# Sixteen repeated semaphore waits at the head of ScalarE's and VectorE's programs

## The chip, the cores and the metric

The kernel runs on one core of one Trainium2 chip. The metric is the device time of one execution in microseconds (us). The median of three runs of the kernel before is 160.86 us (160.74 to 161.05).

## The reference

```python
def reference(x):                     # x: 32 x 512 x 1024, float32
    relu_x = np.maximum(x, 0)
    return np.sum(relu_x, axis=-1).astype(np.float32)   # 32 x 512
```

Seen as a matrix, x has 16384 rows of 1024 numbers, 64 MiB in all. Each row's positive numbers are summed to one number. There is no matrix product: the work is to read 64 MiB once, and to make one pass of relu and one pass of summing over it.

## The kernel before, in words

**Tiling.** The 16384 rows are laid over the 128 partitions, 128 rows for each partition. The work goes by "rows of a partition": one such row is a piece of 128 partitions x 1024 numbers, 512 KB. There are 7 big chunks of 16 rows (`CHUNKS`, 8 MB each), then a tail of 8, 4 and 2 rows (`TAIL`), and then the last two rows, which are cut into four small pieces (`first`, `second`, `third` and the `seam` tile), so that little work is left when the last bytes arrive.

**Loads.** All loads are DMAs that SyncE (SP) issues on one queue. The buffer `buf` has three slots (`NB = 3`) of 16 rows. Chunk 0 is loaded by two DMAs (1 row and 15 rows) on the same semaphore, `s_in[0]`, so that chunk 0 has landed when `s_in[0]` is at 32; the kernel moves these two issues ahead of the core's opening barrier (L95 to L97). Chunks 1 and 2 follow at once. From chunk 3 on, the issue at L91 waits at L87 until VectorE has finished the chunk that used the slot (`s_dve` at `done[c - NB]`). The tail's issues (L101), the pieces of the last rows (L112) and the seam (L115) come behind the wait for VectorE's end of chunk 4.

**Work.** For chunks 0 to 5 ScalarE (ACT) does relu in place in large ACTIVATEs (L145, one ACTIVATE for the whole of chunk 0, then steps of 7 and 9 rows and smaller), and each raises `s_act`. VectorE (DVE) waits for `s_act` (L159) and sums the rows with TENSOR_REDUCE (L160), each raising `s_dve`. Of chunk 5, four rows are done with relu and sum in one instruction: two on ScalarE by `on_act` (L127), two on VectorE by `on_dve` (L130). From chunk 6 on, nothing passes between the two engines any more: they take alternate rows, each with relu and sum in one instruction. At the very end both wait for the seam and for each other's halves (L199 to L203), SP stores the last results (L207), and waits until the stores have landed (L209).

**Order at the start.** ScalarE's first instruction of the kernel's body is the table load for relu, put in by the compiler (it shows as ACT_TABLE_LOAD under L145). Then comes the ACTIVATE of chunk 0, which itself carries the wait of L140 for `s_in[0]` at 32. VectorE's first instruction is the first TENSOR_REDUCE of chunk 0, which carries the wait for `s_act` at 1. Each engine takes its own instructions in order.

A wait that is followed by an instruction of its engine rides on that instruction; where there are more waits than one, the compiler makes EVENT_SEMAPHORE instructions of them, which only wait, two waits to one instruction (L122 and L209 are such pairs on SP).

Of the kernel before, what the change touches and what calls it, by code (L numbers as in the profile page):

```python
# [8 lines left out]
CHUNKS = [[(0, 0, 1), (1, 0, 15)]] + [[(1, 16 * c + 15, 16)] for c in range(6)]  # L9
# [2 lines left out]
TAIL = [8, 4, 2]  # L12
CUT = 912
HEAD = 256


def bass_relu_sum_kernel(
# [19 lines left out]
    B, S, _ = x.shape  # L37
# [14 lines left out]
    w = D - CUT  # L52
    seam = nc.alloc_sbuf_tensor("seam", [P, 2 + w + HEAD + 2], fp32)
    res = nc.alloc_sbuf_tensor("res", [P, J], fp32)
# [3 lines left out]
    s_in = [nc.alloc_semaphore(f"s_in{i}") for i in range(n_in)]  # L58
# [11 lines left out]
    sp, act, dve = nc.sync, nc.scalar, nc.vector  # L70
# [38 lines left out]
    flat = buf[:, tb, r : r + 2, :].rearrange("p j d -> p (j d)")  # L109
    first, second, third = [(0, CUT), (D + D // 2, 2 * D), (D + HEAD, D + D // 2)]  # L110
    for k, (lo, hi) in enumerate((first, second, third)):
        sp.dma_start(out=flat[:, lo:hi], in_=rows[:, lo:hi]).then_inc(  # L112
            s_in[NBIG + len(TAIL) + k], 16
        )
    sp.dma_start(out=seam[:, 2 : 2 + w + HEAD], in_=rows[:, CUT : D + HEAD]).then_inc(s_seam, 16)  # L115
    sp.wait_ge(s_turn, 1)
# [9 lines left out]
    def on_act(t, acc):  # L126
        return act.activation(t, t, AF.Relu, accum_out=acc)  # L127

    def on_dve(t, acc):
        return dve.tensor_scalar(  # L130
            out=t, in0=t, scalar1=0.0, scalar2=None, op0=ALU.max, op1=ALU.add, accum_out=acc
        )

    def row(c, i):
        return buf[:, c % NB, i, :], res[:, c * BIG + i : c * BIG + i + 1]

    k = 0
    for c in range(NTWO):
        alone = BIG - sum(ACT_STEPS[c])
# [54 lines left out]
    act.wait_ge(s_in[-2], 16)  # L194
    on_act(flat[:, lo:hi], seam[:, k + HEAD : k + HEAD + 1]).then_inc(s_seam, 1)
    lo, hi = third
    dve.wait_ge(s_in[-1], 16)
    on_dve(flat[:, lo:hi], seam[:, k + HEAD + 1 : k + HEAD + 2]).then_inc(s_seam, 1)
    act.wait_ge(s_seam, 16 + 2)  # L199
    act.wait_ge(s_half, 2)  # L200
    on_act(seam[:, 0:k], res[:, J - 2 : J - 1]).then_inc(s_last, 1)
    dve.wait_ge(s_seam, 16 + 2)
    on_dve(seam[:, k : k + HEAD + 2], res[:, J - 1 : J]).then_inc(s_last, 1)  # L203

# [33 lines left out]
```

## Time and profile before

| What | Value |
|---|---|
| median of 3 runs | 160.86 us (160.74 to 161.05) |
| profiled execution: span, first to last instruction | 159.4 us |
| profiled execution: last semaphore record of the closing barrier, from the span's start | 160.85 us |
| DVE busy | 120.6 us (76%), 59 instructions |
| ACT busy | 101.5 us (64%), 54 instructions |
| loads and stores (q1), share of 16 DMA engines | 98.1% |
| HBM read | 67.11 MB, 421 GB/s over the span |
| code (q14) within the span | 1 packet of 8192 bytes, at 159.21 us |

The page's span goes from SP's first DMA issue to SP's last wait. Behind it lies the closing of the program: the engines meet in a barrier, clear their semaphores and meet once more. The last record of this in the trace is at 160.85 us, 1.46 us behind the span's end, so the profiled execution's own time, counted like this, agrees with the median of the runs.

A line such as `137.72 1.22 DVE L130 ... [0.42 <-DMA buf<-in_x_dram]` of the timeline says: at 137.72 us VectorE began an instruction of line 130 that took 1.22 us; the engine was idle for 0.42 us before it, and a load's landing ended that idle time. In the view of waits, the three numbers are the total, the number of waits and the longest. In the table by stretch, the last three columns are the granted clock, the busy share of the DMA engines and GB/s. "q" behind an engine's name means its sequencer, the part that takes the instructions in order and handles waits.

### The profile page before, as it was taken

How to read it: one execution, taken by the hardware profiler on the slowest of the kernel's cores; microseconds unless marked ns; L12 is line 12 of the kernel's file. 1: busy time of each engine (PE TensorE's matmuls, PEld its weight loads, DVE VectorE, ACT ScalarE, POOL GpSimd, SP SyncE). 2: the span in 40 equal slices, each digit the busy share in tenths (PEclk: the TensorE clock that was granted, in tenths of full speed). 3: DMA queues.
4: the chain of work that ended last, by engine and by line, in shares of the span. 5: the costliest groups of instructions: out<-in, count | busy, mean ns of one | idle time of the engine just before them, and what ended most of it. 6: DMA issues, size and time to landing. Idle time of an engine off the chain costs nothing.

```text
span 159.4 us, 150 instructions
## 1 busy us (share of the span) xinstructions
DVE 120.6 (76%) x59; ACT 101.5 (64%) x54; POOL 0.2 (0%) x4
## 2 busy tenths in 40 slices
DVE  0000000009999999999999999999999999898995
ACT  3000059980799708996099941999329980496975
POOL 0000000000000000000000000000000000000000
DMA  9997996996996997989979969969969979798994
GB/s 378 493 401 339 493 526 263 526 526 263 526 493 296 526 444 345 526 378 411 526 312 477 526 263 526 526 263 526 526 263 526 444 345 526 321 469 374 417 400 142
DMA packets 2457, 67.18 MB, mean 421 GB/s; under 512 B 536, under 2 KB 792, under 8 KB 1176
## 3 DMA queue, kind: packets, MB, share of 16 engines
q1 hardware_dynamic: 2456, 67.18, 98.1%
q14 instruction: 1, 0.01, 0.0%
HBM read 67.11 MB, written 0.07 MB: 421 GB/s over the span
## 4 chain that ended last, share of the span: by engine, by line
DVE 55%; DMA 34%; ACT 9%; SPq 2%; issue 0%
DVE res L160 54%; DMA buf<-in_x_dram 34%; ACT buf L145 9%; SPq L101 1%; SPq L112 1%; DVE buf L130 0%; DVE seam L130 0%; SPq L91 0%; DVE turned L169 0%
## 5 line engine op out<-in xcount | busy, mean ns | idle before, releaser
L160 DVE TENSOR_REDUCE res<-buf 128x4 f32<-128x4096 f32 (+3 forms) x18 | 99.4, 5596 | 35.5 <-ACT buf L145 35.5
L145 ACT ACTIVATE buf<-buf 128x7168 f32<-128x7168 f32 (+5 forms) x13 | 80.4, 6233 | 46.1 <-DMA buf<-in_x_dram 46.1
L127 ACT ACTIVATE buf<-buf 128x1024 f32<-128x1024 f32 (+2 forms) x19 | 19.0, 999 | 8.9 <-DMA buf<-in_x_dram 8.9
L130 DVE TENSOR_SCALAR_CACHE_REDUCE buf<-buf 128x1024 f32<-128x1024 f32 (+2 forms) x19 | 20.7, 1143 | 1.7 <-DMA buf<-in_x_dram 1.6
L127 ACT ACTIVATION_READ_ACCUMULATOR buf<-buf 128x1 f32 x19 | 3.6, 188 | 0.0
L145 ACT ACT_TABLE_LOAD x1 | 1.3, 1283 | 1.3 <-PEq L223 1.3
L130 DVE DVE_READ_ACCUMULATOR buf<-buf 128x1 f32 x19 | 1.6, 84 | 0.0
L130 DVE TENSOR_SCALAR_CACHE_REDUCE seam<-seam 128x258 f32<-128x258 f32 x1 | 0.4, 421 | 0.0
L127 ACT ACTIVATE seam<-seam 128x114 f32<-128x114 f32 x1 | 0.3, 300 | 0.1
L169 DVE STREAM_TRANSPOSE turned<-res 128x32 f32<-128x32 f32 x1 | 0.2, 211 | 0.0
L127 ACT ACTIVATION_READ_ACCUMULATOR seam<-seam 128x1 f32 x1 | 0.2, 186 | 0.0
L223 POOL MEMSET const-bfloat16-1.0<- 128x1 bf16 x1 | 0.1, 101 | 0.0
L223 POOL MEMSET const-uint8-127<- 128x1 uint8 x1 | 0.1, 101 | 0.0
L223 POOL MEMSET const-float32-0.0<- 128x1 f32 x1 | 0.1, 98 | 0.2 <-issue 0.2
L223 POOL MEMSET const-float32-1.0<- 128x1 f32 x1 | 0.1, 98 | 0.0
L130 DVE DVE_READ_ACCUMULATOR seam<-seam 128x1 f32 x1 | 0.1, 82 | 0.0
## 6 DMA issues: line engine op xcount, KB each, us to landing
buf<-in_x_dram SPq DMA_DIRECT2D x1, 7680.0 KB, 21.1
buf<-in_x_dram SPq DMA_DIRECT2D x1, 4096.0 KB, 25.3
buf<-in_x_dram SPq DMA_DIRECT2D x1, 2048.0 KB, 29.9
buf<-in_x_dram SPq DMA_DIRECT2D x1, 1024.0 KB, 31.9
buf<-in_x_dram SPq DMA_DIRECT2D x1, 512.0 KB, 3.3
buf<-in_x_dram SPq DMA_DIRECT2D x1, 456.0 KB, 32.5
buf<-in_x_dram SPq DMA_DIRECT2D x1, 256.0 KB, 32.7
seam<-in_x_dram SPq DMA_DIRECT2D x1, 184.0 KB, 32.6
```

The costliest lines, as they stand in the source:

```text
L101: sp.dma_start(out=buf[:, tb, r : r + n, :], in_=xv[-1][:, r : r + n, :]).then_inc(s_in[NBIG + i], 16)
L112: sp.dma_start(out=flat[:, lo:hi], in_=rows[:, lo:hi]).then_inc(s_in[NBIG + len(TAIL) + k], 16)
L127: return act.activation(t, t, AF.Relu, accum_out=acc)
L130: return dve.tensor_scalar(out=t, in0=t, scalar1=0.0, scalar2=None, op0=ALU.max, op1=ALU.add, accum_out=acc)
L145: act.activation(t, t, AF.Relu).then_inc(s_act, 1)
L160: dve.tensor_reduce(out=res[:, c * BIG + r : c * BIG + r + n], in_=buf[:, c % NB, r : r + n, :], axis=X, op=ALU.add,).then_inc(s_dve, 1)
L169: dve.transpose(out=turned[:, :], in_=res[:, 0:32]).then_inc(s_turn, 1)
L223: nc = _bacc.Bacc("TRN2", target_bir_lowering=False, num_devices=1)
```

## The change

A constant `FILL = 16` is added, and, behind the definition of `row` (L134 and L135) and ahead of the loop that emits both engines' work (L138), ScalarE and VectorE get sixteen waits each for `s_in[0]` at 32, that is, for the landing of both loads of chunk 0. They become eight instructions on each engine. ScalarE's own wait of L140 for the same value stays. Nothing else changes.

```diff
+FILL = 16
...
     def row(c, i):
         return buf[:, c % NB, i, :], res[:, c * BIG + i : c * BIG + i + 1]
 
+    for engine in (act, dve):
+        for _ in range(FILL):
+            engine.wait_ge(s_in[0], 16 * len(CHUNKS[0]))
     k = 0
     for c in range(NTWO):
```

## Prediction

> **What bounds the kernel now.** I read the table by stretch first, with cuts where chunks land. Its last columns are clock, DMA share and GB/s.
>
> ```profile
> 21.60:41.00 19.40, 5.50 (x2) 13.89 (x2) 0.00 (x0) 1.00 1.00 432
> 60.30:79.70 19.40, 19.36 (x6) 13.99 (x3) 0.00 (x0) 1.00 1.00 432
> 99.00:118.40 19.40, 19.40 (x5) 14.08 (x4) 0.00 (x0) 1.00 1.00 432
> 147.40:152.30 4.90, 4.65 (x8) 4.27 (x8) 0.00 (x0) 1.00 0.97 416
> ```
>
> The loads run at 432 GB/s with the DMA engines full, early and late. DVE (first number) looks full in the middle too, so the waits have to say which of the two is ahead.
>
> ```profile
> ACT buf L145 <- DMA buf<-in_x_dram: 46.1, 6, 19.1
> DVE res L160 <- ACT buf L145: 35.5, 1, 35.5
> DVE buf L130 <- DMA buf<-in_x_dram: 1.6, 4, 0.5
> ```
>
> ACT waits for a load at every chunk. DVE waits once at the start and then works without a gap, because it starts late and catches up; from chunk 6 on it, too, waits for loads, four times. ACT's timeline gives the pace of the loads:
>
> ```profile
> 1.27 1.28 ACT L145 ACT_TABLE_LOAD   x1 [1.27 <-PEq L223]
> 21.61 13.86 ACT L145 ACTIVATE buf<-buf 128x16384 f32<-128x16384 f32 x1 [19.06 <-DMA buf<-in_x_dram]
> 40.97 13.95 ACT L145 ACTIVATE buf<-buf 128x7168 f32<-128x7168 f32 x2 [5.50 <-DMA buf<-in_x_dram]
> 60.31 13.95 ACT L145 ACTIVATE buf<-buf 128x7168 f32<-128x7168 f32 x2 [5.39 <-DMA buf<-in_x_dram]
> ```
>
> A chunk lands every 19.35 us; ACT needs 13.95 us for one, DVE 17.3 us (52.75 to 70.07). So **the stream of loads sets the end**. The chain of waits puts 54% on DVE's L160, but it follows the tail's issue (L101, at 122.07 us) back to DVE, and that issue had time: the queue was full with chunk 6, which landed at 137.72 us.
>
> **The change, part by part.** Of each engine's sixteen waits, made into eight EVENT_SEMAPHOREs, the first blocks until chunk 0 has landed (21.59 us, the semaphore's last count), so all eight pass after that, in order.
>
> *DVE's eight* cost nothing on the path: behind them stands the first TENSOR_REDUCE, which waits for ACT until 35.50 us anyway. The cover is 13.9 us, against at most 8 x 0.079 = 0.63 us (below).
>
> *ACT's eight* stand ahead of the ACTIVATE of chunk 0, for which DVE waits. The trace of before has no row of such a string on ACT. Bounds for one: below, ACT's only EVENT_SEMAPHOREs last 0.017 us (L223, L200); above, POOL's two at the start begin 0.079 us apart (1.070 and 1.149), the second waiting for nothing. Nearest in kind is SP's L122, with two waits: it begins at 157.005, and the next instruction at 157.080, 0.075 us apart. I take 0.075: 8 x 0.075 = 0.60 us (0.14 to 0.63).
>
> *The table load* is moved by the change, though the diff doesn't name it. Now it runs at 1.27 us, behind ACT's opening barrier and ahead of the ACTIVATE that carries the wait, and is hidden under the first load (19.06 us of idle time follow). It belongs to L145, to the ACTIVATE; the new waits are instructions of their own ahead of that line. I expect the load behind them, in the open: 1.283 us, plus 0.055 us as between ACT's barrier instruction (1.194 + 0.017) and the load (1.266). What passes between a table load's end and an ACTIVATE no row shows, since a wait follows it; at least 0, and, by the longest pause for draining in the trace (POOL's DRAIN), 0.179 us. I take 0.
>
> ```profile
> L145 ACT ACT_TABLE_LOAD  x1: 1283/1283/1283, 1.3 to 1.3; - x1
> ```
>
> The Trainium skill bears on both halves of this. "ScalarE: Activation LUTs", section "Step-by-step: what each stage is for", says that the compiler places the load right before the ACTIVATE that needs it; that speaks against this change. Its section "What ACT_TABLE_LOAD costs" adds a drain of about 1380 ns to the 1283 ns; the trace has the 1283 ns, and no run here shows the other. By that page the sum below would be 3.32 us instead of 1.94, and the time some 162.1 us.
>
> Sum: ACT begins chunk 0 later by 0.60 + 0.06 + 1.28 = **1.94 us** (0.14, if the load stays ahead and each wait costs 0.017, to 0.63 + 0.06 + 1.28 + 0.18 = 2.15).
>
> *Where that goes.* ACT ends chunk 0 at 35.47 + 1.94 = 37.41, ahead of chunk 1 at 40.97: ACT is on time again after one chunk. DVE starts at 35.50 + 1.94 and, having no gap up to 137.2 us, stays 1.94 late. Queued behind it are SP's issues. Chunk 3's, at 52.86 us, goes to 54.8; the queue still holds chunk 2 until 60.3, so the DMA engines don't run dry. The later ones have more room, each chunk 19.35 - 17.3 = 2 us more. Then come DVE's gaps at the end:
>
> ```profile
> 137.72 1.22 DVE L130 TENSOR_SCALAR_CACHE_REDUCE buf<-buf 128x1024 f32<-128x1024 f32 x1 [0.42 <-DMA buf<-in_x_dram]
> ...
> 147.43 1.22 DVE L130 TENSOR_SCALAR_CACHE_REDUCE buf<-buf 128x1024 f32<-128x1024 f32 x1 [0.51 <-DMA buf<-in_x_dram]
> ...
> 152.32 1.22 DVE L130 TENSOR_SCALAR_CACHE_REDUCE buf<-buf 128x1024 f32<-128x1024 f32 x1 [0.24 <-DMA buf<-in_x_dram]
> ...
> 157.01 0.42 DVE L130 TENSOR_SCALAR_CACHE_REDUCE buf<-buf 128x256 f32<-128x256 f32 x1 [0.40 <-DMA buf<-in_x_dram]
> ```
>
> An instruction of DVE can begin 0.08 us before the record of the one ahead ends (39.834 against 35.497 + 4.419). So the gaps are 137.72 - 137.22 = 0.50, 147.43 - 146.85 = 0.58, 152.32 - 152.00 = 0.32, 154.84 - 154.61 = 0.23 and 157.01 - 156.53 = 0.48: together 2.11 us. 1.94 us of delay is used up there, piece by piece, with 0.17 to spare when the third piece lands. The end stays: span 159.4, closing barrier to 160.85. That is the profiled execution's own time; the median of the runs is 160.86. At the upper bound 2.15 - 2.11 = 0.04 us is left over. Without these gaps, the whole 1.94 us would show.
>
> *Code.* Eight instructions more on each engine move all that follows. The trace has one code packet within the span:
>
> ```profile
> q14 instruction: 1, 0.01, 7.7%
> ```
>
> (in the DMA view from 159.0 to 159.4 us): 8192 bytes, begun at 159.212, lasting 0.493 us. I take it to stay off the path, and make it a rival.
>
> **The rivals.**
>
> *1. The load stays ahead of the waits (0.12).* For it: nothing keeps a table load from running early. Against: it bears the ACTIVATE's line. Then the delay is 0.14 to 0.63 us, used up in DVE's first two gaps: 160.86.
>
> *2. Slower: after the table load something is in the way that the trace hides (0.15).* Its place is between the load and the first ACTIVATE; now 19.06 us of idle time cover whatever is there. It decides from 2.11 - 1.94 = 0.17 us on; beyond that, each ns of it is a ns of the end. The far row is the load itself: as long again is 1.283 us, 1.283 - 0.17 = 1.11 us late, 161.97. Over 0.49 us of it the change is slower by over 0.2%.
>
> *3. The code packet comes earlier (0.17).* It begins 1.3 us after DVE's and ACT's last instructions (157.9); SP's DMAs take about a us from issue to their first packet (0.00 to 1.01, 157.93 to 158.77), so it is likely asked for when one of the two leaves its work. Eight instructions earlier on either is about 155.8 us or before, and the packet then falls among the last loads, which land up to 156.99. One of the 16 engines would be busy for 0.493 us with it, and a landing needs all 16. Price 0 to 0.49: up to 161.35. Against: at 156 us little is left on the queue. The skill's "Runtime: NRT & Kernel Launch", "Instruction fetch mechanics", has refills of 16 KiB, mostly hidden; the trace shows 8192 bytes, and by that rule the price would be 0.
>
> *4. Faster: the closing now waits for that packet (0.11).* It ends at 159.705, while the barrier's release runs from 159.51 to 159.67. Asked for earlier, it frees at least 0.19 us (159.705 - 159.51), at most its 0.49: 160.37. Against: the barrier's records follow each other at about 0.04 us, with no hole where one engine is late.
>
> **How the numbers follow.** The likeliest is that ACT's delay is absorbed: 0.45, at 160.86 (to 160.90 at its bounds). Rival 1 adds 0.12 at the same time. About 0.2% (0.32 us) is what a measurement of this kernel can tell from no change. Of rival 3's 0.17, 0.10 are over that, 0.07 not; of rival 4's 0.11, 0.08 and 0.03; rival 2 is over it. Within: 0.45 + 0.12 + 0.07 + 0.03 = 0.67; slower 0.15 + 0.10 = 0.25; faster 0.08. The range goes from 160.5 (rival 4's larger part left out) to 161.5 (rival 3 whole, and the first part of rival 2); what it leaves out is under 0.2.
>
> **What would show it.** Right: ACT_TABLE_LOAD at 22.2 us or so; the first ACTIVATE at 23.5; the first TENSOR_REDUCE at 37.4; ACT's second chunk at 40.97 as before; the waits of L130 on loads down from 1.6 us to near nothing; chunks landing every 19.35 us. Wrong in a step: the load still at 1.27 (rival 1); a hole between load and ACTIVATE (rival 2); q14's packet before 157 us (rival 3); a shorter stretch behind the span (rival 4). The prediction falls altogether if chunks land at another pace, or if DVE loses its 2 us of catching up in a chunk.

## The result

The changed kernel takes 161.55 us (median of 5 runs, 161.41 to 161.69), the kernel before 160.93 us beside it (5 runs). The ratio is 1.0042, 95% interval 1.0029 to 1.0054: slower by 0.62 us. The forecast was no change, 160.86 us, with a range up to 161.5.

The profile after, first the start. Timeline of ScalarE and VectorE, the rows that answer to those at 1.27, 21.61 and 35.50 us before (VectorE's of before stands first, the other two stand in the prediction):

```profile
35.50 34.58 DVE L160 TENSOR_REDUCE res<-buf 128x4 f32<-128x4096 f32 x6 [35.50 <-ACT buf L145]
```

```profile
22.21 1.28 ACT L149 ACT_TABLE_LOAD   x1 [22.21 <-DMA buf<-in_x_dram]
23.50 13.86 ACT L149 ACTIVATE buf<-buf 128x16384 f32<-128x16384 f32 x1
...
37.49 4.42 DVE L164 TENSOR_REDUCE res<-buf 128x4 f32<-128x4096 f32 x1 [37.49 <-ACT buf L149]
```

The table load stands behind the waits, in the open. ScalarE begins 1.89 us late, VectorE 1.99 us. The waits themselves, by line (count, then shortest, median and longest duration in ns, then first and last start in us):

```profile
L140 ACTq EVENT_SEMAPHORE  x7: 38/38/38, 21.6 to 22.1; - x7
L140 DVEq EVENT_SEMAPHORE  x7: 50/50/50, 21.6 to 22.2; - x7
```

(The eighth of each is kept under the line of the wait that it is paired with.) They begin 0.076 us apart on ScalarE and about 0.098 us apart on VectorE.

Now the end: VectorE's rows where it waited for loads before, and the view of waits.

```profile
139.21 1.21 DVE L131 TENSOR_SCALAR_CACHE_REDUCE buf<-buf 128x1024 f32<-128x1024 f32 x1
...
148.32 1.21 DVE L131 TENSOR_SCALAR_CACHE_REDUCE buf<-buf 128x1024 f32<-128x1024 f32 x1
...
152.97 1.22 DVE L131 TENSOR_SCALAR_CACHE_REDUCE buf<-buf 128x1024 f32<-128x1024 f32 x1
...
157.59 0.42 DVE L131 TENSOR_SCALAR_CACHE_REDUCE buf<-buf 128x256 f32<-128x256 f32 x1 [0.35 <-DMA buf<-in_x_dram]
```

```profile
DVE buf L131 <- DMA buf<-in_x_dram: 0.3, 1, 0.3
```

VectorE is 1.49 us late at chunk 6 (139.21 against 137.72), 0.89 us at the tail's first load (148.32 against 147.43), 0.65 us at the second (152.97 against 152.32). The first two steps are what the gaps of 0.50 and 0.58 us were reckoned to take up. But then it stays at about 0.6, and at the third piece (157.59 against 157.01) VectorE *waits* again, for a load that is itself 0.58 us late. ScalarE, which was on time again long before, shows the same on the loads alone:

```profile
137.73 1.06 ACT L128 ACTIVATE buf<-buf 128x1024 f32<-128x1024 f32 x1 [6.65 <-DMA buf<-in_x_dram]
...
148.06 1.06 ACT L128 ACTIVATE buf<-buf 128x1024 f32<-128x1024 f32 x1 [1.91 <-DMA buf<-in_x_dram]
...
152.97 1.06 ACT L128 ACTIVATE buf<-buf 128x1024 f32<-128x1024 f32 x1 [0.63 <-DMA buf<-in_x_dram]
```

The same three before:

```profile
137.72 1.06 ACT L127 ACTIVATE buf<-buf 128x1024 f32<-128x1024 f32 x1 [6.65 <-DMA buf<-in_x_dram]
...
147.43 1.06 ACT L127 ACTIVATE buf<-buf 128x1024 f32<-128x1024 f32 x1 [1.29 <-DMA buf<-in_x_dram]
...
152.32 1.06 ACT L127 ACTIVATE buf<-buf 128x1024 f32<-128x1024 f32 x1 [0.62 <-DMA buf<-in_x_dram]
```

Chunk 6 lands on time, and from the next load on every landing is late, by 0.58 to 0.64 us. Something came between. The page's queues (q14 carries code; before, it had one packet in the span), and the DMA view from 145 to 146 us:

```profile
q14 instruction: 2, 0.02, 0.0%
```

```profile
q14 instruction: 1, 0.01, 1.9%
```

There are two code packets in the span instead of one, and one of them lies **in the middle of the loads**: 8192 bytes, begun at 145.497 us, 0.309 us long (the other begins at 158.318). A 32 KB packet of the loads that begins as the code packet ends (145.802 against 145.806 us) took 1.769 us; those around it took 1.213. A landing raises its semaphore once for each of the 16 DMA engines. The semaphore's records for the third piece of the last rows (`s_in[12]`) show that one engine alone is late, and all wait for it:

```
s_in[12], us of the last three of 16      before: 156.94  156.95  156.99
                                          after:  156.93  156.98  157.57
```

In this profiled execution (161.69 us, the longest of the five) SP's last wait begins 0.93 us later than before (160.295 against 159.366). Of that, VectorE's end makes 0.59 us (158.495 against 157.903), and the other 0.34 us come behind it, with the last store (see e12).

So the question for the chip was: is it this packet, whose packet is it, and does the delay of 1.99 us have a part?

### The profile page after: what moved, and what is told of

Same layout as the page of the kernel before. It is cut to its first block, busy times and chain, and to the rows that moved or that the text cites. A ratio compares the mean times of both kernels' runs of the same rounds, so it can differ in the third digit from the quotient of the medians.

```text
span 160.3 us, 166 instructions
## 1 busy us (share of the span) xinstructions
DVE 120.4 (75%) x59; ACT 101.5 (63%) x54; POOL 0.2 (0%) x4
## 4 chain that ended last, share of the span: by engine, by line
DVE 55%; DMA 33%; ACT 9%; SPq 2%; issue 0%; ACTq 0%; DVEq 0%
DVE res L164 54%; DMA buf<-in_x_dram 33%; ACT buf L149 9%; ACT L149 1%; SPq L102 1%; SPq L113 1%; DVE buf L131 0%; DVE seam L131 0%; SPq L92 0%; ACTq L140 0%; DVE turned L173 0%; DVEq L163 0%; ACTq L144 0%
## 5 line engine op out<-in xcount | busy, mean ns | idle before, releaser
L149 ACT ACT_TABLE_LOAD x1 | 1.3, 1283 | 22.2 <-DMA buf<-in_x_dram 22.2
```

Of the source, the lines that this page charges most:

```text
L149: act.activation(t, t, AF.Relu).then_inc(s_act, 1)
```

## The experiments

Theory C (code): the further instructions move a code packet into the stream of loads; the delay is absorbed. Rival D (delay): the late start is what costs. All ratios are to the kernel before, timed on the same chip beside them, with 95% intervals.

**e1: the waits on ScalarE alone.** **e2: on VectorE alone.** In the added loop:

```diff
-    for engine in (act, dve):
+    for engine in (act,):        # e1
+    for engine in (dve,):        # e2
```

> The sixteen waits on ScalarE alone. Theory C (code): the loss comes from a code packet of 8192 bytes that the eight further instructions of one engine bring into the stream of loads; the 1.99 us of delay are absorbed. Then the time is up by about 0.6 us with a packet before 157 us if the packet belongs to ScalarE's program, and not up at all (within 0.2 us) if it belongs to VectorE's; in both cases the table load is at 22.2 us. Rival D (delay): the 1.99 us by which ScalarE and VectorE begin later are the cause; then up by about 0.6 us whatever the packet does.

> The sixteen waits on VectorE alone; table load at 1.27 us and first TENSOR_REDUCE at 35.5 us as in the kernel before. Theory C: up by about 0.6 us with a packet in the stream if the packet is VectorE's (one of the two engines must have it), else no change. Rival D: no change, since nothing begins later.

e1: 161.03 us, ratio 1.0011 (1.0002 to 1.0020). e2: 161.53 us, ratio 1.0047 (1.0033 to 1.0060). e2 has the whole loss with nearly nothing of the delay: table load at 1.27 us, the first ACTIVATE at 21.59, the first TENSOR_REDUCE at 35.58. Its only code packet begins at 143.105 us, and there is none at 159. Timeline of ScalarE in e2:

```profile
137.76 1.06 ACT L128 ACTIVATE buf<-buf 128x1024 f32<-128x1024 f32 x1 [6.65 <-DMA buf<-in_x_dram]
148.11 1.06 ACT L128 ACTIVATE buf<-buf 128x1024 f32<-128x1024 f32 x1 [1.92 <-DMA buf<-in_x_dram]
```

Again on time at chunk 6, and late by 0.68 us from the next load on. e1 has the whole delay (first ACTIVATE at 23.63 us), no packet among the loads, and 0.18 us of loss. Its packets begin at 158.439 and 159.618 us. So the packet at 159.2 us in the kernel before is VectorE's, and ScalarE's eight instructions bring in one of ScalarE's at about 158.4. Theory C holds for the main part; rival D doesn't.

**e3: eight instructions more on each engine, but early ones.** A scratch tile `go` is written by GpSimd, which raises `s_go`; the added loop becomes

```diff
...
+    pool.memset(go[:, :], 0.0).then_inc(s_go, 1)
+    for _ in range(15):
+        act.wait_ge(s_go, 1)
+    act.activation(go[:, 0:1], go[:, 0:1], AF.Relu)
+    for _ in range(15):
+        dve.wait_ge(s_go, 1)
+    dve.memset(go[:, 1:2], 0.0)
```

> Eight further instructions on each engine, but none that delays: fifteen waits for a semaphore that GpSimd raises at the start, and one tiny instruction (a relu or memset of one column of a scratch tile), all done by about 4 us; the first large ACTIVATE at 21.6 us as in the kernel before. Theory C: a code packet near 145 us, loads of the tail about 0.6 us late, time up by 0.6 us. Rival D: no change.

161.43 us, ratio 1.0040 (1.0028 to 1.0053). Timeline of ScalarE at the start, and the DMA view from 143 to 144 us:

```profile
1.93 1.28 ACT L144 ACT_TABLE_LOAD   x1 [1.93 <-POOL go L141]
3.23 0.20 ACT L144 ACTIVATE go<-go 128x1 f32<-128x1 f32 x1
21.65 13.86 ACT L156 ACTIVATE buf<-buf 128x16384 f32<-128x16384 f32 x1 [18.22 <-DMA buf<-in_x_dram]
```

```profile
q14 instruction: 1, 0.01, 2.1%
```

All of the added work is over at 3.4 us, chunk 0 begins when it did before, and the loss is there in full, with the packet at 143.222 us.

**e4: the delay without the instructions.** ScalarE's wait for chunk 0 goes by way of GpSimd, which first writes a scratch tile; no instruction more on ScalarE or VectorE.

```diff
...
+    pool.wait_ge(s_in[0], 16 * len(CHUNKS[0]))
+    pool.memset(pause[:, :], 0.0).then_inc(s_go, 1)      # pause: 128 x 1900
...
-        act.wait_ge(s_in[c], 16 * len(CHUNKS[c]))
+        act.wait_ge(s_go, 1)                             # for c == 0
```

> The delay without the instructions: no further waits; ScalarE's first ACTIVATE waits for a GpSimd memset of a scratch tile that begins when chunk 0 has landed, about 1.6 to 2 us of delay; ScalarE and VectorE have as many instructions as in the kernel before, table load at 1.27 us. Theory C: one code packet, behind the loads, no change (within 0.2 us); VectorE's gaps at the end take the delay up. Rival D: up by about 0.6 us.

160.80 us, ratio 1.0001 (0.9993 to 1.0010). The start, by the timeline, and VectorE's waits:

```profile
23.41 13.86 ACT L153 ACTIVATE buf<-buf 128x16384 f32<-128x16384 f32 x1 [20.86 <-POOL pause L141]
```

```profile
DVE buf L130 <- DMA buf<-in_x_dram: 0.3, 1, 0.3
```

A late start of 1.80 us costs nothing: VectorE's waits for loads at the end shrink from 1.6 to 0.3 us, and the third piece's semaphore is complete at 157.04 us (156.99 before).

**e5, e6, e7: 2, 4 and 24 instructions more on VectorE alone**, made as VectorE's part of e3 (with 3, 7 and 47 waits).

> Two further instructions on VectorE alone (one pair of waits for GpSimd's early semaphore and one tiny memset), done by about 3 us. The packet's place should go by the number of instructions ahead: at 0 it began at 159.2 us, at 8 at 143 to 145 us. If it moves in step, it begins between 155 and 159 us here, where only the small last loads or the stores are left: 0 to 0.4 us. If the place is a matter of the number of instructions passing a border at once, it is either at 159 (no change) or near 145 (up by 0.6 us).

> Four further instructions on VectorE, early. In step: the packet begins between 147 and 156 us, that is in the stream of loads, and the time is up by 0.4 to 0.6 us. By a border: as at 2 or as at 8.

> 24 further instructions on VectorE, early. In step: the packet begins well before 143 us, between 100 and 135 us, while VectorE does the large sums; the price stays at about 0.6 us, for the DMA engine that is late by it has no idle time in which to catch up. If the price were one of the tail alone (small pieces), it would be gone here.

All three lose the same: 161.44 us (1.0037, 1.0024 to 1.0049), 161.46 us (1.0037, 1.0024 to 1.0051) and 161.42 us (1.0040, 1.0027 to 1.0053). The packets, and the last two of the third piece's 16 semaphore records, from the traces:

```
kernel       more on DVE   VectorE's packet, us   s_in[12], last two, us
before            0             159.21                156.95  156.99
e5                2             151.67                157.00  157.70
e6                4             151.08                157.03  157.66
after             8             145.50                156.98  157.57
e2                8             143.11                157.02  157.61
e3                8             143.22                157.03  157.82
e7               24             127.87                157.36  158.08
```

More instructions ahead bring the packet earlier, though not by an even step: between 0 and 2 it moves by 7.5 us, from behind the loads to their midst, between 2 and 4 by 0.6. For e5 my expectation of 155 to 159 us was wrong, and so was that of a smaller loss there. The price is the same at all these places in the stream: one engine of 16 is late by 0.6 to 0.8 us in each, and doesn't catch up before the last landing. In each of the six traces with a packet among the loads, one load packet, begun within 0.02 us of the code packet's end, took 0.53 to 0.66 us longer than others of its size; in the traces of the kernel before and of e11, below, no load packet after the first 10 us is longer by as much as 0.15 us. (In e7's profiled execution the whole stream is also about 0.35 us late, before the packet as well.)

**e8: VectorE's sixteen waits behind its last work** instead of ahead of its first:

```diff
     on_dve(seam[:, k : k + HEAD + 2], res[:, J - 1 : J]).then_inc(s_last, 1)
+    for _ in range(FILL):
+        dve.wait_ge(s_in[0], 16 * len(CHUNKS[0]))
```

> VectorE's sixteen waits (eight instructions) behind its last work instead of ahead of its first: as many instructions, as long a program. If what counts is how many instructions stand ahead of the work, the packet is asked for at the end of VectorE's work or behind it, as in the kernel before (158 us or later), and the time is up by less than 0.25 us. If the length of the program counts, the packet is near 145 us and the time up by 0.6 us.

The packet is back at 159.251 us and the loads are undisturbed (third piece complete at 157.08 us): what sets its place is the number of instructions ahead. But the time is 161.82 us, ratio 1.0063 (1.0051 to 1.0076), so that expectation failed. SP's waits tell where:

```profile
SPq L212 <- DMA out_dram<-res: 2.3, 1, 2.3
```

SP now waits 2.3 us for the last store to land. Before, it was 1.1 us:

```profile
SPq L209 <- DMA out_dram<-res: 1.1, 1, 1.1
```

15 of its 16 engines are done at 159.43 us, the 16th at 160.63: on that engine the store's eight packets of 64 bytes begin at 159.611 us, right behind the code packet (159.251 + 0.364), while on the others they are over at 159.05. In the kernel before, a code packet at nearly the same time (159.212) came behind the store's packets. Why that engine took none of them between 158.85 and 159.25 us the trace doesn't show.

**e9: the pause of e4, longer** (3400 elements instead of 1900).

> The pause on GpSimd alone again, with a memset of 3400 elements for each partition instead of 1900, so a delay of about 3.2 us instead of 1.82 us; no instruction more on ScalarE and VectorE. VectorE's gaps at the end were reckoned to take up 2.11 us. If that sum is right, the end is later by 3.2 - 2.1 = 1.1 us, with the landings where they were. If VectorE's delay is taken up in another way (loads issued later and faster, say), no change; if the gaps are worth less than 1.8 us, more than 1.4 us.

161.67 us, ratio 1.0044 (1.0032 to 1.0057), 0.76 us above the kernel before. VectorE begins 3.16 us late (38.66 us) and reaches its last instruction 1.01 us late (158.48 against 157.47), so 3.16 - 1.01 = 2.15 us were taken up in this execution, against the 2.11 reckoned. The time by the runs, 0.5 to 0.9 us above, is a little under the 1.05 us that 3.16 - 2.11 gives.

**e10: the changed kernel whole, with VectorE's program as long as before**, by larger sums. **e11: the same shorter program without the waits.**

```diff
-DVE_STEPS = [[4, 5, 7], [7, 4, 5], [7, 4, 5], [7, 4, 5], [4, 5, 7], [3, 4, 5]]
+DVE_STEPS = [[16], [16], [7, 9], [7, 9], [9, 7], [7, 5]]
```

> The changed kernel whole, with the same delay, but VectorE's sums of chunks 0 to 5 in 10 TENSOR_REDUCEs instead of 18, so that VectorE's program is as long as in the kernel before. Theory C: VectorE's packet is back behind the loads (158 us or later), the loads of the tail land as in the kernel before, and of the 0.6 us at least 0.4 are gone (160.85 to 161.1 us, the rest being ScalarE's packet). If the position of VectorE's packet is not the cause, the time stays at 161.5 us.

> The kernel before with VectorE's 10 TENSOR_REDUCEs instead of 18, no waits added: eight instructions fewer. Theory C: VectorE's packet is asked for still later in the closing or not at all; no loss, and a gain only if the packet behind the loads costs something now: within 0.3 us of the kernel before.

e10: 160.89 us, ratio 0.9998 (0.9990 to 1.0007). The loss is gone, with the waits, the exposed table load and the delay still there:

```profile
22.25 1.28 ACT L149 ACT_TABLE_LOAD   x1 [22.25 <-DMA buf<-in_x_dram]
23.54 13.86 ACT L149 ACTIVATE buf<-buf 128x16384 f32<-128x16384 f32 x1
...
147.47 1.06 ACT L128 ACTIVATE buf<-buf 128x1024 f32<-128x1024 f32 x1 [1.28 <-DMA buf<-in_x_dram]
152.36 1.06 ACT L128 ACTIVATE buf<-buf 128x1024 f32<-128x1024 f32 x1 [0.62 <-DMA buf<-in_x_dram]
```

Its code packets begin at 158.240 and 159.335 us, behind the loads, and the loads land as before the change. e11: 160.86 us, ratio 0.9996 (0.9987 to 1.0005); no code packet lies within its span at all. So the packet at 159.2 us cost the kernel before nothing that these runs can tell, and nothing is won by moving it further.

**e12: eight early instructions on ScalarE alone** (ScalarE's part of e3).

> Eight further instructions on ScalarE alone, all done by 4 us, so without the delay. With the waits in place on ScalarE alone the time was up by 0.18 us. If ScalarE's packet among the last stores does that, it is up by about 0.2 us here too; if the 2 us of delay do it, no change.

160.90 us, ratio 0.9998 (0.9989 to 1.0007): no change, with ScalarE's packet at 157.757 us. So neither eight instructions on ScalarE by themselves (e12) nor the delay by itself (e4) makes e1's 0.18 us. In e1's profiled execution one engine of 16 ends the last store late (159.79 us, the others by 159.49), with ScalarE's packet at 158.439; in that of the changed kernel ten of 16 end it at 160.16 to 160.28, the others by 159.83, with the packet at 158.318 and 0.559 us long. That fits the case of e8, on a smaller scale, but e10, with the packet at 158.240, shows no loss. What this packet costs, and when, stays open; it is at most a small part.

No kernel here beats the one before: the best (e4, e10, e11, e12) equal it.

## Why the prediction was wrong, point by point

- **The bound** was right: the loads set the end, and the main part of the loss is a loss of the loads.
- **ACT's eight waits**, 0.075 us apiece: measured 0.076. **The table load** behind the waits: right, at 22.21 us (forecast 22.2). **Between load and ACTIVATE** I took 0: 23.504 - (22.209 + 1.283) = 0.012 us. The drain of about 1380 ns from the Trainium skill's "ScalarE: Activation LUTs", "What ACT_TABLE_LOAD costs", doesn't show here, where nothing runs ahead of the load; the forecast by the row was the better one. Rival 2 is out. What the page's section "Step-by-step: what each stage is for" says of the place of the load, right before the ACTIVATE, is what the trace shows. Sum forecast 1.94, measured 1.89 us.
- **DVE's eight at nothing**: off by 0.10 us. The first TENSOR_REDUCE's own wait for ScalarE was paired into the eighth EVENT_SEMAPHORE (it passes at 37.396 us), and the sum begins 0.09 us behind it instead of at once (e2: 35.58 against 35.50). It was absorbed with the rest.
- **The gaps of 2.11 us**: right. e4 loses nothing at 1.80 us, and e9 takes up 2.15 of 3.16 us.
- **"Code. ... I take it to stay off the path"**: this is the step that failed. The packet moved to 145.5 us, into a stream that had no idle time, and its price was the result. Rival 3 had the mechanism, at a chance of 0.17, and was wrong in place and size. I put the packet at 155.8 us or before by counting eight instructions back from the end of the work; it came 10 us earlier, when 25 of VectorE's 69 recorded instructions had yet to begin. And I priced it by its own duration, up to 0.49 us; in the stream it lasted only 0.309 us, but the engine that took it fell behind by 0.6 to 0.8 us, most of it in one load packet, which was stretched by 0.556 us (1.769 against 1.213). Why that is more than the code packet's own 0.309 us the trace doesn't show. "At 156 us little is left on the queue", my argument against it, fell with the place. So it is the cost put at 0 that failed: e2, with VectorE's packet alone, loses 0.68 us (161.53 against 160.85), and e10, with that packet moved back, loses nothing. What ScalarE's packet among the last stores adds to the 0.62 us of the changed kernel stays open (e1: 0.18 us, e12: none).
- The rule of the skill's "Runtime: NRT & Kernel Launch", "Instruction fetch mechanics", that refills are mostly hidden, held for the engine that gets the code: neither engine shows a hole. It did not hold for the loads that share the DMA engines. Each packet in the span was of 8192 bytes, and VectorE's came singly; no block of 16 KiB shows.
- **Rival 4** (the closing waits for the packet) is out: e11 has no packet there and is not faster.

## What to carry to other kernels

Where the DMA engines are full to the end, count what else rides on them: one 8 KB code packet on one of 16 engines cost 0.6 us here, because every landing waits for the slowest engine. Instructions that cost an engine nothing can still move that packet, so look at the code queue's packets in the trace before and after a change of the number of instructions, and if one falls into the stream, make the program of that engine as much shorter ahead of the work that runs when the packet comes (e10 got all of it back). In this kernel, whose loads kept their pace, a late start cost its length less the consumer's gaps further on (nothing for 1.80 us in e4; 3.16 - 2.15 = 1.01 us at VectorE's last instruction in e9), and those gaps could be summed from the timeline beforehand.

## What the runs showed that I had not expected

- Two instructions more on VectorE moved its code packet by 7.5 us (159.21 to 151.67), and 24 by 31 us (to 127.87): how far ahead code is asked for is not settled by these runs. When the packet began among the loads, VectorE had begun 42 to 52 of its recorded instructions and had 13 (e5, e6) to 37 (e7) still to begin; in the kernel before it had begun all 61.
- A code packet that meets a small store can cost more than one among the loads: in e8 the last store landed 1.20 us after its other 15 engines (160.63 against 159.43), behind a packet of 0.364 us.
